# Twenty of the 22 hidden row tiles of a gated feed-forward product computed by Strassen's scheme

## The chip, the cores and the metric

The kernel runs on one core of one Trainium2 chip. The metric is the time of one execution on the device in microseconds (us), as the median of several runs. A difference under about 0.2% (1.6 us) can't be told from no change.

The engines are named as the profile names them: PE is TensorE (matmuls), PEld its weight loads, DVE is VectorE, ACT is ScalarE, POOL is GpSimd, SP is SyncE, whose queue issues most transfers.

## The reference, cut to what matters

One layer of a transformer on 512 tokens of 1024 channels in float32: a mixer of four branches, and then a feed-forward part.

```python
def _swiglu(x, w_in, w_out):
    g, u = jnp.split(x @ w_in, 2, axis=-1)
    return (jax.nn.silu(g) * u) @ w_out

for l in range(DEPTH):
    xn = _rms_norm(h, norm_mix_g[l])
    h = h + _mixer_block(xn, ...)
    h = h + _swiglu(_rms_norm(h, norm_ffn_g[l]), w_ffn_in[l], w_ffn_out[l])
```

`w_ffn_in` is 1024 x 5632 (2816 gate columns, then 2816 up columns), `w_ffn_out` 2816 x 1024. The change touches the feed-forward part alone, and the pools that its tiles lie in.

## The kernel before

Activations stand transposed: 128 channels on the partitions, 512 tokens along. Every float32 operand is kept as two float32r parts, a high one (an ACT copy) and a low one (the source less the high part, on DVE); `split` (lines 119 to 121) makes them. A product of two operands is three matmuls, high by high, high by low, low by high (`mm3`, lines 132 to 134), each of 128 x 128 weights over 512 columns.

All weights of the feed-forward part come as a stream of 128 x 128 units, eight to a chunk of 512 KB, in the order of their use (`unit_stream`, `next_unit`). `load_units` loads a chunk by a transfer on SP's queue (line 146) into one of three `raw` buffers and splits it into `whi` (3 buffers) and `wlo` (2 buffers). Hidden row tile j takes 8 units of the gate columns and 8 of the up columns: 16 units, 48 matmuls.

The mixer ends with `w_out` (line 691); its results are `h1` (tiles `mrg`), and `hg`, which is `h1` times the second norm's gain, in parts (tiles `xg`). The norm itself, `r2`, comes from a sum over channels (`rms`, lines 251 to 261) and is multiplied in only after the products: `gp` by `r2` (line 715), Silu on ACT (716), by `r2` again (717), by `up` (721). So the feed-forward part's matmuls follow those of `w_out` without a wait for `r2`. The 22 row tiles are done in two halves of 11; after each half the eight blocks of `w_ffn_out` take the half's hidden rows (33 matmuls a block) and add to `h1` (731).

The program is written in the order above, and a scheduler then sets the order of each engine's instructions when the program is built. On the chip each engine and each queue takes its instructions in that order. A tile's buffer is taken again when the last reader of the tile before is done; the instruction or transfer that fills it waits for that reader.

Of the kernel before, what the change touches and what calls it, by code (L numbers as in the profile page):

```python
# [29 lines left out]
FH = FK // 2  # L30
# [10 lines left out]
# columns of the packed small parameters  # L41
# [5 lines left out]
# the order of the blocks of forgetting attention's q and k, which VectorE works on for long, and of the convolution  # L47
# [3 lines left out]
def unit_stream():  # L51
    """The 128x128 weight units in the order in which the kernel uses them: (matrix, row tile, column)."""
    s = []

    def block(m, col, ks):
        for k in ks:
            s.append((m, k, col))
# [13 lines left out]
    for half in range(2):  # L71
        ks = range(half * FH, (half + 1) * FH)
        for j in ks:
            block("w_ffn_in", j * P, range(KT))
            block("w_ffn_in", FFN + j * P, range(KT))
        for d in range(KT):
            block("w_ffn_out", d * P, ks)
    return s

# [6 lines left out]
def mixer_kernel(ctx, tc, xT, units, wt1, wt2, wsT, small, out):  # L86
# [5 lines left out]
    slots = ctx.enter_context(tc.tile_pool(name="slots", bufs=1))  # L92
# [3 lines left out]
    BUFS = dict(xg=16, y=18, att=4, aug=6, mrg=8, tmp=6, gt=4)  # L96
# [6 lines left out]
    def slot(tag, dtype=F32):  # L103
        return slots.tile([P, T], dtype, tag=tag, bufs=BUFS[tag], name=nm(tag))
# [62 lines left out]
    # the activation table that Copy and Square are taken from  # L167
# [16 lines left out]
    def x_parts(k):  # L184
        x_k, g = xs[k][:, 0:T], xs[k][:, T:T + 1]
        hi, lo = slot("xg", F32R), slot("xg", F32R)
# [23 lines left out]
    # tri[s, t] = 1 where s <= t  # L210
# [3 lines left out]
    # ntri[s, t] = -1 where s >= t  # L214
# [11 lines left out]
    # mask_sb[k, q] = NEG where k >= q; mask_fx[q, k] = NEG where k > q  # L226
# [10 lines left out]
    # the mean over a head's channels  # L237
# [65 lines left out]
    def token_group(wt, width, nk, banks):  # L303
        """The products of the tokens with a weight of `width` columns; nk row tiles to a chunk."""
        for c in range(KT // nk):
# [3 lines left out]
            lo = wpool.tile([P, nk * width], F32R, tag="wlo", bufs=2, name=nm("wlo"))  # L309
# [9 lines left out]
    def v_parts(banks, first, name):  # L319
        """A head's values in their two parts side by side, so that one product takes both."""  # L320
# [13 lines left out]
    # gmlp's v: gelu, layer norm  # L334
# [22 lines left out]
    # gmlp's causal weights, [s, g, t], kept where s <= t  # L357
# [96 lines left out]
    # log of the forget gate, -softplus(-x), and its sums over the tokens  # L454
# [5 lines left out]
    def values(h, v, wh, wl, w3, dst):  # L460
# [10 lines left out]
        # the lower half has the products of the values' low part  # L471
# [9 lines left out]
    def sb_scores(h):  # L481
# [4 lines left out]
        # both parts of k over the high part of q twice; the high part of k over the low part of q  # L486
# [37 lines left out]
        # in place of row tile 2 its sum with row tile 3, in place of 1 its sum with 2 and 3  # L524
# [7 lines left out]
        # w = exp(z - the sums of softplus over the keys from this one on)  # L532
# [40 lines left out]
    # rows that carry the sums into the products of q and k: 1, 1, F of the query in two parts over  # L573
    # F of the key in two parts, negated, 1, 1
# [19 lines left out]
    def fox_head(h):  # L594
# [4 lines left out]
        # both parts of q over the high part of k twice; the high part of q over the low part of k, and the sums  # L599
# [56 lines left out]
    # sigmoid(x) = (1 + tanh(x / 2)) / 2, of which the last half is taken in at the end  # L656
# [26 lines left out]
    h1, hg = [], []  # L683
    hsum = slot("tmp")
    for d in range(KT):
# [8 lines left out]
        hi, lo = slot("xg", F32R), slot("xg", F32R)  # L694
# [12 lines left out]
    for half in range(2):  # L707
        ks = range(half * FH, (half + 1) * FH)
        a = {}
        for j in ks:  # L710
            gp = bank("g")
            for k in range(KT):
                mm3(gp, next_unit(("w_ffn_in", k, j * P)), hg[k], k == 0, k == KT - 1)
            t = slot("gt")
            V.tensor_tensor(t, gp, r2, op=ALU.mult)  # L715
            S.activation(t, t, AF.Silu)
            V.tensor_tensor(t, t, r2, op=ALU.mult)
            up = bank("g")
            for k in range(KT):
                mm3(up, next_unit(("w_ffn_in", k, FFN + j * P)), hg[k], k == 0, k == KT - 1)  # L720
            V.tensor_tensor(t, up, t, op=ALU.mult)  # L721
            a[j] = tuple(slot("att" if j - ks[0] < 2 else "y", F32R) for _ in range(2))
            split(*a[j], t)
# [13 lines left out]
def pack(inputs):  # L737
    """The inputs in the order in which the program reads them."""
# [50 lines left out]
```

## Time and profile before

| what | value |
|---|---|
| time, median of 3 runs | 824.54 us (823.51 to 824.6) |
| span of the profiled execution, first to last instruction | 821.7 us |
| the rest of the median, before and after the span | 2.8 us |
| PE busy | 816.3 us, 99% of the span |
| DVE, ACT busy | 453.7 us (55%), 322.6 us (39%) |
| POOL busy | 2.4 us |
| bytes moved by transfers | 78.88 MB, mean 96 GB/s |

The profile gives the profiled execution's span; its time as a run isn't listed apart, and the three runs lie 1.8 to 2.9 us above the span. A matmul's shown duration holds its way through the array and overlaps the next one's, so the time that a matmul takes of PE is the distance from its start to the next one's start. DVE's instructions overlap by some 0.08 us in the same way.

### The profile page before, as it was taken

What the parts mean: (1) busy time and instruction counts of PE and PEld (TensorE: products, weight loads), DVE (VectorE), ACT (ScalarE), POOL (GpSimd) and SP (SyncE); (2) the same over time, 40 slices, a digit from 0 to 9 for tenths busy, and PEclk for the clock granted to TensorE, in tenths of its full rate; (3) what the DMA queues carried; (4) which work ended last, traced back from release to release, by engine and by line L of the source; (5) the groups of instructions that cost most, each with busy time, mean ns of one, the idle gap of its engine ahead of it and who ended that gap; (6) DMA issues with size and microseconds to landing.
All of it is one profiled execution on the core that took longest, in us unless ns stands there. A gap on an engine that the chain in (4) does not pass through costs nothing.

```text
span 821.7 us, 9248 instructions
## 1 busy us (share of the span) xinstructions
PE 816.3 (99%) x3653; PEld 658.8 (80%) x3653; DVE 453.7 (55%) x711; ACT 322.6 (39%) x485; POOL 2.4 (0%) x11
## 2 busy tenths in 40 slices
PE   9999999999999999999999999999999999999998
PEld 6888897777788888878888888888888888888886
DVE  8438895776577788756555443444333344344222
ACT  7336337576545455434344432232122233223210
POOL 0000000000000000000000000000000000000000
PEclk9999999999999999999999999999999999999999
DMA  7232321221222222213352223223322222322331
GB/s 286 93 103 91 102 78 58 97 63 66 77 78 80 89 84 69 91 64 103 103 185 85 93 88 102 103 78 102 103 98 83 102 89 92 102 96 84 128 116 39
DMA packets 24091, 78.88 MB, mean 96 GB/s; under 512 B 2672, under 2 KB 2928, under 8 KB 24048
## 3 DMA queue, kind: packets, MB, share of 16 engines
q1 hardware_dynamic: 22608, 75.80, 27.3%
q10 hardware_dynamic: 1440, 2.49, 0.9%
q8 instruction: 29, 0.48, 0.2%
q14 instruction: 14, 0.11, 0.0%
HBM read 76.18 MB, written 2.10 MB: 95 GB/s over the span
## 4 chain that ended last, share of the span: by engine, by line
PE 99%; DVE 0%; DVEq 0%; issue 0%
PE ps L134 30%; PE ps L132 29%; PE ps L133 29%; PE ps L128 1%; PE ps L129 1%; PE ps L130 1%; PE ps L467 1%; PE ps L632 1%; PE ps L502 1%; PE ps L171 0%; PE ps L616 0%; PE ps L469 0%; PE ps L617 0%; PE ps L501 0%; PE ps L537 0%; PE ps L536 0%
## 5 line engine op out<-in xcount | busy, mean ns | idle before, releaser
L132 PE MATMUL ps<-xg,whi 128*128 128x512 f32 x736 | 290.3, 396 | 0.0
L133 PE MATMUL ps<-xg,whi 128*128 128x512 f32 x736 | 289.8, 395 | 0.0
L134 PE MATMUL ps<-xg,wlo 128*128 128x512 f32 x736 | 288.6, 395 | 0.4 <-DVE wlo L121 0.4
L120 ACT ACTIVATE whi<-raw 128x1024 fp32r<-128x1024 f32 (+1 forms) x140 | 144.7, 1034 | 349.5 <-issue 182.2
L121 DVE TENSOR_TENSOR wlo<-raw,whi 128x1024 fp32r<-128x1024 f32 (+1 forms) x140 | 166.4, 1189 | 88.8 <-PE ps L134 68.5
L134 PEld LDWEIGHTS ps<-xg,wlo 128*128 128x128 f32 x736 | 138.3, 188 | 32.6 <-DVE wlo L121 0.8
L132 PEld LDWEIGHTS ps<-xg,whi 128*128 128x128 f32 x736 | 138.5, 188 | 32.1 <-ACT whi L120 0.8
L133 PEld LDWEIGHTS ps<-xg,whi 128*128 128x128 f32 x736 | 138.5, 188 | 31.4 <-issue 0.5
L134 PE MATMUL ps<-y,wlo 128*128 128x512 f32 x256 | 101.1, 396 | 0.0
L132 PE MATMUL ps<-y,whi 128*128 128x512 f32 x256 | 100.8, 394 | 0.3 <-DVE gt L671 0.3
L133 PE MATMUL ps<-y,whi 128*128 128x512 f32 x256 | 101.0, 394 | 0.0
L132 PEld LDWEIGHTS ps<-y,whi 128*128 128x128 f32 x256 | 48.1, 188 | 11.8 <-DVE gt L671 0.8
L134 PEld LDWEIGHTS ps<-y,wlo 128*128 128x128 f32 x256 | 48.1, 188 | 11.2 <-issue 0.3
L133 PEld LDWEIGHTS ps<-y,whi 128*128 128x128 f32 x256 | 48.0, 188 | 11.3 <-issue 0.2
L715 DVE TENSOR_TENSOR gt<-ps,r 128x512 f32<-128x512 f32 x22 | 15.2, 691 | 65.6 <-PE ps L134 63.7
L721 DVE TENSOR_TENSOR gt<-ps,gt 128x512 f32<-128x512 f32 x22 | 15.2, 692 | 65.2 <-PE ps L134 65.2
L662 DVE TENSOR_TENSOR gt<-ps,r 128x512 f32<-128x512 f32 x32 | 22.1, 690 | 25.3 <-PE ps L134 25.3
L663 ACT ACTIVATE gt<-gt 128x512 f32<-128x512 f32 x32 | 20.1, 630 | 37.9 <-DVE gt L662 37.9
L731 DVE TENSOR_TENSOR mrg<-ps,mrg 128x512 f32<-128x512 f32 (+1 forms) x17 | 11.1, 659 | 34.4 <-PE ps L134 34.2
L129 PE MATMUL ps<-whi,xg 128*128 128x512 f32 (+1 forms) x64 | 21.6, 338 | 0.0
L128 PE MATMUL ps<-whi,xg 128*128 128x512 f32 (+1 forms) x64 | 21.5, 338 | 0.0
L130 PE MATMUL ps<-wlo,xg 128*128 128x512 f32 (+1 forms) x64 | 21.3, 337 | 0.0
(229 smaller groups left out, 688.9 us busy)
## 6 DMA issues: line engine op xcount, KB each, us to landing
raw<-units SPq DMA_DIRECT2D x126, 512.0 KB, 3.2
x<-xT SPq DMA_DIRECT2D x8, 256.5 KB, 5.3
raw<-units SPq DMA_DIRECT2D x8, 256.0 KB, 5.3
raw<-wt SPq DMA_DIRECT2D x4, 512.0 KB, 3.2
tmp<-xT ACTq DMA_DIRECT2D x8, 256.0 KB, 4.3
outT<-mrg SPq DMA_DIRECT2D x7, 256.0 KB, 2.0
raw<-wt SPq DMA_DIRECT2D x2, 520.0 KB, 3.2
sml<-small SPq DMA_DIRECT2D x1, 394.0 KB, 5.7
```

Of the source, the lines that this page charges most:

```text
L120: S.activation(dst_hi, src, AF.Copy)
L121: V.tensor_tensor(dst_lo, src, f(dst_hi), op=ALU.subtract)
L128: PE.matmul(out=ps, lhsT=ah, rhs=bh, start=start, stop=False)
L129: PE.matmul(out=ps, lhsT=al, rhs=bh, start=False, stop=False)
L130: PE.matmul(out=ps, lhsT=ah, rhs=bl, start=False, stop=stop)
L132: PE.matmul(out=ps, lhsT=ah, rhs=bh, start=start, stop=False)
L133: PE.matmul(out=ps, lhsT=ah, rhs=bl, start=False, stop=False)
L134: PE.matmul(out=ps, lhsT=al, rhs=bh, start=False, stop=stop)
L662: V.tensor_tensor(t, proj_block(OFF["gate"] + n * D + d * P), r1, op=ALU.mult)
L663: S.activation(t, t, AF.Tanh, scale=0.5)
L715: V.tensor_tensor(t, gp, r2, op=ALU.mult)
L721: V.tensor_tensor(t, up, t, op=ALU.mult)
```

## The change

The gate and up columns of row tiles 2 to 21 are taken two row tiles at a time. For such a pair (a "quad" in the code) the weight is a matrix of 2 x 2 blocks, B11 and B21 the gate columns of the lower and the upper 512 channels, B12 and B22 the up columns. The activations are a 2 x 2 matrix too, by halves of the tokens (256) and halves of the channels. Strassen's scheme in Winograd's form makes the four result blocks from seven block products instead of eight. A block product is 24 matmuls of 256 columns (`product`), so a pair takes 168 matmuls of 256 columns where it took 96 of 512.

The scheme needs sums of blocks. Of the weights, for each pair: t1 = B12 + B11, t2 = t1 + B22, t3 = B12 + B22, t4 = t2 + B21 (the signs of the scheme lie in the activations' sums s1 to s4 and in the subtractions of results). t2 and t4 are made on DVE (`quad_sum`). t1 and t3 are made by two transfers each (`quad_loaded_sum`): SP's queue loads one block into a buffer of the pool `sum`, and when it has landed a transfer from POOL's queue adds the other block to it. All seven operands, summed or not, are then split. Of the activations the sums s1 to s4 and the parts of seven operands (tiles `op`) are made once, ahead of the first pair; they need the normed activations, so `r2` comes in ahead of the products (the tiles A, line 773).

Row tiles 0 and 1 (PLAIN) stay as they were and come first. `w_ffn_out` is now taken in three groups, after 8, 16 and 22 hidden row tiles. `wlo` has 3 buffers instead of 2. The pool `sum` has 6 buffers: the two PLAIN row tiles' hidden parts take two until the first `w_ffn_out` group has read them, and s1 to s4 the other four.

```diff
+PLAIN = 2
+GROUPS = (8, 8, 6)
@@
+def quad_stream():
+    return [(j, half, side) for j in range(PLAIN, FK, 2) for half, side in ((0, 0), (0, 1), (1, 1), (1, 0))]
@@
-                         wpool.tile([P, UNITS * P], F32R, tag="wlo", bufs=2, name=nm("wlo")))
+                         wpool.tile([P, UNITS * P], F32R, tag="wlo", bufs=3, name=nm("wlo")))
@@
+    mix.close()
+    ffn = ctx.enter_context(tc.tile_pool(name="ffn", bufs=1, reuse_waits="tile"))
+    H = T // 2
+    hidden = {}
+    for j in range(PLAIN):
...
+        a = ffn.tile([P, 2, T], F32R, tag="sum", bufs=6, name=nm("plain"))
+        hidden[j] = (a[:, 0], a[:, 1])
+        split(*hidden[j], t)
+    def block4(tag, dtype=F32, bufs=5):
+        return ffn.tile([P, 4, H], dtype, tag=tag, bufs=bufs, name=nm(tag))
+    A = {}
     for half in range(2):
+        A[0, half], A[1, half] = block4("sraw"), block4("sraw")
+        for k in range(4):
+            d = 4 * half + k
+            g = sml[:, C_G2 + d:C_G2 + d + 1]
+            for th in range(2):
+                ts = slice(th * H, (th + 1) * H)
+                V.scalar_tensor_tensor(A[th, half][:, k], h1[d][:, ts], g, r2[:, ts], op0=ALU.mult, op1=ALU.mult)
+    def operand(src):
+        hi, lo = block4("op", F32R, 14), block4("op", F32R, 14)
+        split(hi, lo, src)
+        return hi, lo
+    def combined(a, b, op):
+        t = block4("sum", F32, 6)
+        V.tensor_tensor(t, a, b, op=op)
+        return t
+    o11, o12, o22 = operand(A[0, 0]), operand(A[0, 1]), operand(A[1, 1])
+    s1 = combined(A[1, 0], A[1, 1], ALU.subtract)
+    s2 = combined(s1, A[0, 0], ALU.subtract)
+    s3 = combined(A[0, 0], A[1, 0], ALU.subtract)
+    s4 = combined(A[0, 1], s2, ALU.add)
+    o1, o2, o3, o4 = operand(s1), operand(s2), operand(s3), operand(s4)
+    def quad(c):
+        raw = ffn.tile([P, UNITS * P], F32, tag="sraw", bufs=5, name=nm("sraw"))
+        nc.sync.dma_start(out=raw, in_=quads[c])
+        return raw
+    def quad_sum(a, b):
+        t = ffn.tile([P, UNITS * P], F32, tag="sum", bufs=6, name=nm("sum"))
+        V.tensor_tensor(t, a, b, op=ALU.add)
+        return t
+    def quad_loaded_sum(a, b):
+        t = ffn.tile([P, UNITS * P], F32, tag="sum", bufs=6, name=nm("sum"))
+        nc.sync.dma_start(out=t, in_=quads[a])
+        G.dma_start(out=t, in_=quads[b], accum_op=ALU.add)
+        return t
+    def product(ps, w, x, first=False):
+        (wh, wl), (xh, xl) = w, x
+        for jj in range(2):
+            dst = ps[:, jj * H:(jj + 1) * H]
+            for k in range(4):
+                u = slice((jj * 4 + k) * P, (jj * 4 + k + 1) * P)
+                ends = k == 3 and jj == 1
+                PE.matmul(out=dst, lhsT=wh[:, u], rhs=xh[:, k], start=first and k == 0 and jj == 0, ...)
+                PE.matmul(out=dst, lhsT=wh[:, u], rhs=xl[:, k], ...)
+                PE.matmul(out=dst, lhsT=wl[:, u], rhs=xh[:, k], ...)
+    def quad_rows(j):
+        c = QUADS.index((j, 0, 0))
+        b11, b22, b21 = quad(c), quad(c + 2), quad(c + 3)
+        ra, rc, rb, rd = (bank("a") for _ in range(4))
+        product(ra, quad_parts(b11), o11, True)
+        p1 = slot("tmp")
+        S.activation(p1, ra, AF.Copy)
+        t1 = quad_loaded_sum(c + 1, c)
+        product(rc, quad_parts(t1), o1, True)
+        t2 = quad_sum(t1, b22)
+        product(rb, quad_parts(t2), o2, True)
+        u = slot("tmp")
+        V.tensor_tensor(u, rb, p1, op=ALU.add)
+        product(ra, quad_parts(b21), o12)
...
+        t3 = quad_loaded_sum(c + 1, c + 2)
+        product(rb, quad_parts(t3), o3)
+        v = slot("tmp")
+        V.tensor_tensor(v, rb, p1, op=ALU.add)
...
+        t4 = quad_sum(t2, b21)
+        product(rd, quad_parts(t4), o22, True)
...
+        product(rc, quad_parts(b22), o4)
```

The seven products of a pair are called P1 to P7 below, in this order: B11 by o11, t1 by o1, t2 by o2, B21 by o12, t3 by o3, t4 by o22, B22 by o4. Each pair has further 9 instructions of 512 columns on DVE: u and v, three sums out of PSUM, two products with the gate and two low parts.

The order on three engines, where the first pair begins. On DVE before, behind PLAIN's place, the work of further row tiles follows (`gt` a row tile's gate, `att` and `y` hidden parts):

```order
L715 TENSOR_TENSOR gt_718_3909<-ps_714_3878,r2_3805 128x512
L121 TENSOR_TENSOR wlo_728_3952<-raw_726_3950,whi_727_3951 128x1024
L121 TENSOR_TENSOR att_713_3875<-gt_707_3838,att_712_3874 128x512
L717 TENSOR_TENSOR gt_718_3909<-gt_718_3909,r2_3805 128x512
L721 TENSOR_TENSOR gt_718_3909<-ps_719_3913,gt_718_3909 128x512
L121 TENSOR_TENSOR wlo_733_3987<-raw_731_3985,whi_732_3986 128x1024
```

On DVE now (`sraw_707` to `710` are the four A tiles, `sum_717`, `718`, `719`, `720` are s1 to s4, `op_722` is o1's low part, `sum_739` is the first pair's t1, `sum_742` its t2, `sraw_730` its B22):

```order
L146 TENSOR_TENSOR plain_706_3935<-gt_701_3899,plain_706_3935 128x512
L782 TENSOR_TENSOR sum_718_3972<-sum_717_3970,sraw_707_3938 128x1024
L782 TENSOR_TENSOR sum_719_3974<-sraw_707_3938,sraw_708_3939 128x1024
L146 TENSOR_TENSOR op_722_3979<-sum_717_3970,op_721_3978 128x1024
L782 TENSOR_TENSOR sum_720_3976<-sraw_709_3948,sum_718_3972 128x1024
L146 TENSOR_TENSOR op_724_3983<-sum_718_3972,op_723_3982 128x1024
L146 TENSOR_TENSOR op_726_3987<-sum_719_3974,op_725_3986 128x1024
L146 TENSOR_TENSOR op_728_3991<-sum_720_3976,op_727_3990 128x1024
L801 TENSOR_TENSOR sum_742_4065<-sum_739_4034,sraw_730_3996 128x1024
L146 TENSOR_TENSOR wlo_741_4038<-sum_739_4034,whi_740_4037 128x1024
```

What is new is all of the rows but the first: the activations' sums and splits stand ahead of t2 and of t1's low part. On SP's queue before, each row loads the next chunk when its buffer is free:

```order
L146 DMA raw_715_3879<-units 128x1024 [waits DMAHW2_49,DMAHW6_49,DVE_49,Activation_49]
L146 DMA raw_720_3914<-units 128x1024 [waits DMAHW4_49,DMAHW7_49,DVE_49,Activation_49]
L146 DMA raw_726_3950<-units 128x1024 [waits DMAHW5_49,DVE_49,Activation_49]
L146 DMA raw_731_3985<-units 128x1024 [waits DMAHW1_49,DMAHW6_49,DVE_49,Activation_49]
L146 DMA raw_737_4021<-units 128x1024 [waits DMAHW7_49,DVE_49,Activation_49]
```

On SP's queue now (`sraw_729`, `730`, `731` are B11, B22, B21 of the first pair, `sraw_763`, `764` B11 and B22 of the second, `sum_739` and `sum_750` t1 and t3 of the first, `sum_773` t1 of the second):

```order
L796 DMA sraw_729_3994<-quads 128x1024 [waits PE_49]
L796 DMA sraw_730_3996<-quads 128x1024 [waits DMAHW4_49,DMAHW3_49,DVE_49]
L796 DMA sraw_731_3998<-quads 128x1024 [waits DVE_49,Activation_49]
L796 DMA sraw_763_4233<-quads 128x1024 [waits DVE_49]
L796 DMA sraw_764_4235<-quads 128x1024
L807 DMA sum_739_4034<-quads 128x1024 [waits DMAHW0_49,DVE_49]
L796 DMA sraw_765_4237<-quads 128x1024 [waits DMAHW1_49,DVE_49]
L807 DMA sum_750_4128<-quads 128x1024 [waits DMAHW2_49,DVE_49]
L807 DMA sum_773_4273<-quads 128x1024 [waits DMASW0_49,DVE_49]
```

The load of t1 stands behind the next pair's blocks. `sum_739` lies in the buffer of s1, so its wait for DVE is for the last reader of s1, the row `op_722` above; `sraw_763` waits for s3, the row `sum_719`. `sum_773` lies in the buffer of `sum_739` and waits for the row `wlo_741`. On PE before, plain row tiles follow each other:

```order
L132 MATMUL ps_719_3913<-xg_698_3786,whi_721_3915 128x512
L133 MATMUL ps_719_3913<-xg_699_3787,whi_721_3915 128x512
L134 MATMUL ps_719_3913<-xg_698_3786,wlo_722_3916 128x512
L132 MATMUL ps_725_3949<-xg_642_3500,whi_727_3951 128x512
L133 MATMUL ps_725_3949<-xg_643_3501,whi_727_3951 128x512
```

On PE now, from the end of P1 (`ps_732`) to the begin of P2 (`ps_733`), with two matmuls of P3 (`ps_734`) between:

```order
L825 MATMUL ps_732_4000<-op_711_3958,whi_736_4004 128x256
L826 MATMUL ps_732_4000<-op_712_3959,whi_736_4004 128x256
L827 MATMUL ps_732_4000<-op_711_3958,wlo_737_4005 128x256
L825 MATMUL ps_733_4001<-op_721_3978,whi_740_4037 128x256
L826 MATMUL ps_733_4001<-op_722_3979,whi_740_4037 128x256
L825 MATMUL ps_734_4002<-op_723_3982,whi_743_4067 128x256
L826 MATMUL ps_734_4002<-op_724_3983,whi_743_4067 128x256
L827 MATMUL ps_733_4001<-op_721_3978,wlo_741_4038 128x256
```

Behind P1 nothing stands on PE that doesn't need t1, and 36 matmuls of PLAIN stand between the last matmul of `rms` and P1.

## Rows read from the trace of the kernel before

**Rows 1.** The page, part 1: busy time, share of the span, instructions.

```profile
PE 816.3 (99%) x3653; PEld 658.8 (80%) x3653; DVE 453.7 (55%) x711; ACT 322.6 (39%) x485; POOL 2.4 (0%) x11
```

**Rows 2.** The page, part 4: the chain that ended last, by engine.

```profile
PE 99%; DVE 0%; DVEq 0%; issue 0%
```

**Rows 3.** Busy time by stretch: the feed-forward part, 260-column matmuls, the kernel's start.

```profile
core 0: us, PE busy (x) PEld busy (x) DVE busy (x) ACT busy (x) POOL busy (x), PEclk, DMA share, GB/s
464.00:821.70 357.70, 354.28 (x1532) 287.31 (x1531) 139.81 (x167) 89.64 (x107) 0.00 (x0) 1.00 0.28 94
113.02:122.96 9.94, 9.94 (x85) 9.89 (x84) 9.78 (x12) 2.98 (x6) 0.00 (x0) 1.00 0.32 106
1.20:5.20 4.00, 3.95 (x10) 1.25 (x10) 3.01 (x19) 2.35 (x4) 1.21 (x5) 1.00 0.64 213
```

**Rows 4.** Timeline (start, duration): the norm inside the first row tiles, last matmul.

```profile
463.48 1.06 PE L258 MATMUL ps<-ident,rc 128*128 128x128 f32 x8
464.29 0.48 PE L132 MATMUL ps<-xg,whi 128*128 128x512 f32 x1
...
465.20 0.69 DVE L715 TENSOR_TENSOR gt<-ps,r 128x512 f32<-128x512 f32 x1 [1.93 <-ACT r L261]
...
817.89 0.40 PE L134 MATMUL ps<-y,wlo 128*128 128x512 f32 x1
```

**Rows 5.** Timeline of PE: matmuls of 256 and of 260 columns.

```profile
110.66 0.28 PE L436 MATMUL ps<-big,vg 128*128 128x256 f32 x1
110.77 0.28 PE L437 MATMUL ps<-big,vg 128*128 128x256 f32 x1
110.89 0.28 PE L438 MATMUL ps<-big,vg 128*128 128x256 f32 x1
111.01 0.28 PE L128 MATMUL ps<-whi,xg 128*128 128x260 f32 x1
...
113.02 0.28 PE L129 MATMUL ps<-whi,xg 128*128 128x260 f32 x1
...
122.84 0.28 PE L130 MATMUL ps<-wlo,xg 128*128 128x260 f32 x1
```

**Rows 6.** Groups of weight loads: those of lines 128 to 130, count, mean ns.

```profile
L129 PEld LDWEIGHTS ps<-whi,xg 128*128 128x128 f32 x64 | 12.0, 188 | 1.5
```

**Rows 7.** Timeline of DVE: back-to-back instructions of 256, 512 and 1024 columns.

```profile
71.58 0.87 DVE L353 SCALAR_TENSOR_TENSOR tmp<-tmp,var,sml 128x256 f32<-128x256 f32 x2
72.37 0.75 DVE L354 TENSOR_TENSOR tmp<-tmp,sml 128x256 f32<-128x256 f32 x2
...
74.99 0.68 DVE L401 TENSOR_TENSOR gt<-ps,r 128x512 f32<-128x512 f32 x1
75.59 1.21 DVE L121 TENSOR_TENSOR wlo<-raw,whi 128x1024 fp32r<-128x1024 f32 x1
76.72 0.75 DVE L121 TENSOR_TENSOR vg<-tmp,vg 128x256 fp32r<-128x256 f32 x2
```

**Rows 8.** Groups on ACT: the high part of a chunk.

```profile
L120 ACT ACTIVATE whi<-raw 128x1024 fp32r<-128x1024 f32 x130 | 137.6, 1059 | 342.7 <-issue 182.2 <-PE ps L133 134.4 <-PE ps L129 12.8
```

**Rows 9.** The page, parts 3 and 6: SP's queue; transfers, KB, us to landing.

```profile
q1 hardware_dynamic: 22608, 75.80, 27.3%
...
raw<-units SPq DMA_DIRECT2D x126, 512.0 KB, 3.2
...
sml<-small SPq DMA_DIRECT2D x1, 394.0 KB, 5.7
```

**Rows 10.** Timeline of PE at the kernel's start, after PE stood idle.

```profile
1.25 3.94 PE L171 MATMUL ps<-tmp 128*128 128x512 bf16 x9 [1.25 <-DVE one L166]
```

**Rows 11.** The chain that ended last, its only long pieces not on PE.

```profile
364.92 0.69 DVE gt L671
365.60 1.15 DVE wlo L121
```

More of the change, by code (lines that the diff above doesn't have):

```diff
@@ L70, in unit_stream, with hidden_groups @@
         block("w_out", d * P, range(KT))
[L71 to L75, printed above, removed]
+    for first, n in hidden_groups():
+        if not first:
+            for j in range(PLAIN):
+                block("w_ffn_in", j * P, range(KT))
+                block("w_ffn_in", FFN + j * P, range(KT))
         for d in range(KT):
-            block("w_ffn_out", d * P, ks)
+            block("w_ffn_out", d * P, range(first, first + n))
     return s
+def hidden_groups():
+    first = 0
+    for n in GROUPS:
+        yield first, n
+        first += n
+    assert first == FK
+def quad_stream():
+    return [(j, half, side) for j in range(PLAIN, FK, 2) for half, side in ((0, 0), (0, 1), (1, 1), (1, 0))]
 STREAM = unit_stream()
@@ L103, in slot, with two @@
     def slot(tag, dtype=F32):
-        return slots.tile([P, T], dtype, tag=tag, bufs=BUFS[tag], name=nm(tag))
+        return (keep if tag in KEEP else slots).tile([P, T], dtype, tag=tag, bufs=BUFS[tag], name=nm(tag))
+    def two(dtype=F32R):
+        return keep.tile([P, 2, T], dtype, tag="xg", bufs=8, name=nm("xg"))
     def big(dtype=F32):
@@ L185, in x_parts @@
         x_k, g = xs[k][:, 0:T], xs[k][:, T:T + 1]
-        hi, lo = slot("xg", F32R), slot("xg", F32R)
+        x2 = two()
+        hi, lo = x2[:, 0], x2[:, 1]
         if k:
@@ L704, in mixer_kernel @@
     _, r2 = rms(hsum, "r2")
-    for half in range(2):
[L708 to L723, printed above, removed]
+    mix.close()
@@ new lines, in quad_parts @@
+    def quad_parts(src):
+        hi = wpool.tile([P, UNITS * P], F32R, tag="whi", name=nm("whi"))
+        lo = wpool.tile([P, UNITS * P], F32R, tag="wlo", bufs=3, name=nm("wlo"))
+        split(hi, lo, src)
+        return hi, lo
+    def product(ps, w, x, first=False):
[5 more added lines that the diff above has]
+                ends = k == 3 and jj == 1
+                PE.matmul(out=dst, lhsT=wh[:, u], rhs=xh[:, k], start=first and k == 0 and jj == 0, stop=False, skip_group_check=True)
+                PE.matmul(out=dst, lhsT=wh[:, u], rhs=xl[:, k], start=False, stop=False, skip_group_check=True)
+                PE.matmul(out=dst, lhsT=wl[:, u], rhs=xh[:, k], start=False, stop=ends, skip_group_check=True)
@@ L724, in mixer_kernel @@
+    for first, n in hidden_groups():
+        ks = range(first, first + n)
+        for j in ks[::2]:
+            if j not in hidden:
+                quad_rows(j)
+        last = ks[-1] == FK - 1
         for d in range(KT):
-            ps = bank("a")
+            ps = bank("g")
             for j in ks:
-                mm3(ps, next_unit(("w_ffn_out", j, d * P)), a[j], j == ks[0], j == ks[-1])
-            parts = 2 if half and d == KT - 1 else 1
+                mm3(ps, next_unit(("w_ffn_out", j, d * P)), hidden[j], j == ks[0], j == ks[-1])
+            parts = 2 if last and d == KT - 1 else 1
@@ L731, in mixer_kernel @@
                 V.tensor_tensor(h1[d][:, cs], ps[:, cs], h1[d][:, cs], op=ALU.add)
-                if half:
+                if last:
                     (nc.scalar if i else nc.sync).dma_start(out=out[d * P:(d + 1) * P, cs], in_=h1[d][:, cs])
@@ L748, in pack @@
         units[c, :, j * P:(j + 1) * P] = mats[m][k * P:(k + 1) * P, col:col + P]
+    quads = np.stack([np.concatenate(
+        [w["w_ffn_in"][k * P:(k + 1) * P, side * FFN + jj * P:side * FFN + (jj + 1) * P]
+         for jj in (j, j + 1) for k in range(4 * half, 4 * half + 4)], axis=1) for j, half, side in quad_stream()])
     def cols(*names):
```

46 lines of the change are left out of this document (39 added, 7 removed).

## The prediction

> **What bounds the kernel now.** I read the page's busy line first [rows 1]: PE 99% of 821.7 us, DVE 55%, ACT 39%, POOL nothing. The chain that ended last is PE for 99% [rows 2]; its only long pieces elsewhere are one gate and one split in the mixer, about 1 us of PE's idle time [rows 11]. So the kernel is bound by the number of columns that PE streams, and a change helps as far as it takes columns away without leaving PE to wait. By stretch [rows 3], the feed-forward part is PE without a gap, at a granted clock of 1.00, with DVE busy 139.8 of 357.7 us (39%) and 28% of the transfers' time used. DVE and the queues have room there, but at the part's begin everything that is new hangs on `r2`, which DVE first reads at 465.20 [rows 4].
>
> **Prices.** In the row tiles PE takes a 512-column matmul each (817.89 - 464.29) / 1526 = 0.2317 us [rows 4]. 256-column ones start (111.01 - 110.66) / 3 = 0.117 us apart, 260-column ones (122.84 - 113.02) / 82 = 0.1198 [rows 5]; I take 0.118. DVE from start to start: 0.40 for 256 columns (71.58 to 72.37 for two), 0.60 for 512, 1.13 for 1024 [rows 7]. ACT takes 1.06 for the high part of a chunk [rows 8]. A 512 KB load lands 3.2 us after issue; SP's queue moved 75.80 MB in 27.3% of 821.7 us, 338 GB/s, so 1.55 us of those 3.2 are bytes and 1.65 a fixed part [rows 9].
>
> **Matmuls: -24.2 us.** A pair took 96 x 0.2317 = 22.24 us and takes 168 x 0.118 = 19.82. That is -2.42 a pair, and there are ten pairs. The columns fall by an eighth (96 x 512 to 168 x 256), the time by 10.9%, since a narrow matmul costs a little more than half of a wide one. Everything below is set against this.
>
> **First wait, low part of o11: +3.1.** The PLAIN row tiles cover PE for 36 x 0.2317 = 8.3 us, to 472.6. P1's second matmul reads o11's low part. DVE from 465.2 does one product with `r2` (0.60), 16 products of 256 columns for the tiles A (6.4), two more of 512 (1.20) and two of 1024 (2.26): 475.7. So PE idles 3.1.
>
> **Second wait, t1: +20.0 (15.7 to 25.9).** P1's other 23 matmuls end at 475.7 + 2.7 = 478.4, and by the order on PE nothing else can run that doesn't need t1. The load of t1 takes s1's buffer, whose last reader is `op_722`, in DVE's queue behind the A tiles, 8 rows of 1024 and 8 of 512 in all: 465.2 + 4.8 + 6.4 + 9.0 = 485.4. On SP's queue it stands behind two loads of the next pair, which wait for `sum_719` and go out at 484.3. It lands behind their bytes at 484.3 + 1.65 + 3 x 1.55 = 490.6, or at 488.6 if it doesn't share with them. Then POOL's transfer adds the other block. No row shows such a transfer. From below it is bounded by a plain load, 3.2; from above by twice the 5.7 us of the slowest landing of such a size [rows 9], 11.4. I take 5.5: the fixed part and the bytes twice, since it must read what it adds to, is 1.65 + 2 x 1.55 = 4.75, and other loads run beside it. A plain load is the nearest row, so I stay nearer to it. t1 stands at 496.1; t2 on DVE and t1's low part take 1.13 each, to 498.4. From 478.4 that is 20.0 us of idle PE. With 3.2 and 488.6 it is 15.7, with 11.4 it is 25.9.
>
> The Trainium skill, "DMA: Bandwidth & Descriptors", section "Anatomy of one DMA", fits a transfer issued from GpSimd with 2.0 us and the bytes at 436 GB/s; an estimate from it is 3.2 us for 512 KB, by which this wait would be 17.7 and the whole kernel about 824. The same page's "Rules for kernel authors" says that an accumulating transfer reads its destination and writes it later, which speaks against taking it for a plain one. No row here shows either.
>
> **Third wait, the second pair's t1: +2.3 (0.1 to 8.2).** That load takes the first t1's buffer when its low part is made, 498.4; load and adding are 3.2 + 5.5, to 507.1. On DVE the second pair's t2 (1.13) stands ahead of u (0.60), which frees the PSUM bank that the first pair's t3 product takes; that is 508.8. PE has P2 to P4 (72 x 0.118 = 8.5 us, a few of them done ahead of t1's low part) until 506.5. PE is slower for a while after an idle stretch: nine matmuls at the kernel's start took 3.94 us, 0.438 each instead of 0.2317 [rows 10], so a few us of cold matmuls lie inside this wait and are no term of their own.
>
> **Fourth wait, behind the first `w_ffn_out` group: +3.6 (1.1 to 9.5).** The load of the t1 after next wants a buffer that a PLAIN row tile's hidden part holds until that group's last matmul. From there 0.2 + 3.2 + 5.5 = 8.9, and three rows of DVE (3.4) ahead of what PE needs: 12.3. PE has P1 to P3 and a little, 8.7. The third group needs no such buffer.
>
> **In the steady pairs: 0, but narrowly.** A pair's t1 load, its adding transfer and the six 1024-column and six 512-column rows of DVE that stand in that ring make 8.9 + 6.8 + 3.6 = 19.3 us, against 19.82 of PE. Above an adding transfer of about 6.0 every us costs one per pair, for nine pairs. DVE has 9 x 1.13 + 9 x 0.60 = 15.6 us per pair, 79%; ACT seven splits (7.4) and about five narrower ones, under 13 us; transfers seven of 512 KB, five plain (7.75 us) and two adding. None of them is the bound by itself.
>
> **Costed at nothing.** The third `w_ffn_out` group's eight extra sums (0.60 each on DVE) lie under blocks of 24 x 0.2317 = 5.56 us. Behind the last pair's P7 the program has 32 matmuls of earlier hidden row tiles (7.4 us), under which its last hidden parts are made (one row of 1024 at most and four of 512 on DVE, about 3.5 us; that is what they would cost uncovered). `wlo`'s third buffer and the pools by tiles touch the mixer only at its 1 us of waits [rows 11]: 0, within 1 either way.
>
> **The sum.** -24.2 + 3.1 + 20.0 + 2.3 + 3.6 = +4.8 against the span of 821.7: 826.5. The median of before lies 2.8 above its span, so 829.3.
>
> **Rivals.**
> *The adding transfer costs no more than a plain one, and the kernel is faster.* Then the third wait is gone but for the cold matmuls, which it no longer covers, 9 x (0.438 - 0.2317) = 1.9, and the waits are 3.1 + 15.7 + 1.9 + 1.1 = 21.8. The sum is -2.4: 822.1. From an adding transfer of about 3.5 us down, with t1's load not held by its neighbours, the sign turns. For it: bytes are idle 72% of the time [rows 3]. Against: what it has to read twice.
> *The ring binds.* At 8 us the waits are 3.1 + 22.5 + 4.8 + 6.1 = 36.5 and the ring adds 2.0 x 9 = 18: +30.3, 854.8. For it: the margin is only half a us a pair. Against: most of the 3.2 us of a landing is fixed part, which needn't double. At 11.4 it would be 5.9 x 3 of waits and 5.4 x 9 of ring above my forecast, about 895.
> *PE doesn't go faster with narrow matmuls, since a weight load takes longer than one.* A weight load is shown as 0.188 us [rows 6]; a matmul of 256 columns that waits for its load would take 0.225 us, 0.118 plus the 0.107 that 128 columns take by the same pitch, and 1680 of them 180 us more: about 1010. Against it: in the stretch of 260 columns 84 loads of 0.188 us (15.8 us) lie within 9.94 us, and the matmuls start 0.1198 apart [rows 3, 5, 6], so loads overlap both matmuls and each other.
>
> The Trainium skill, "TensorE: Matmul & The Clock Gate", Part 3, "The mechanism", holds that a weight load runs beside matmuls in flight only where it takes another row group of the array; all of this kernel's take the whole array, so by it the last rival would come true. The trace disagrees: 0.1198 us apart with a load for every matmul.
>
> **How the numbers follow.** The forecast (adding transfer 4 to 6.5 us) has 0.5, the plain price 0.27, the binding ring 0.16, the weight loads 0.01, anything else 0.06. A measurement of this kernel can tell about 0.2%, 1.6 us, from no change: faster is below 822.9, slower above 826.2. At an adding transfer of 4 the waits are 3.1 + 18.5 + 1.9 + 2.1 = 25.6, 825.9 in all; at 6.5 there are 3 more of waits and 4.5 of ring, 836.8. So 0.44 of the forecast's 0.5 is slower and 0.06 the same. Of the plain price 0.21 is faster and 0.06 the same (with t1's load behind its neighbours it is about 824). Of the rest 0.04 is faster, by waits shorter than I summed them, 0.01 the same, and 0.18 slower with the ring and the weight loads. Faster 0.25, the same 0.13, slower 0.62. The range reaches down to the plain price with 6 us less of waits, a third of the second one (816), and up to an adding transfer of 7.5: 829.3 + 3 x 2.0 + 9 x 1.5 = 848.8, so 850.
>
> **What would show it.** Right: matmuls of 256 columns 0.117 to 0.120 us apart in the pairs; one gap of PE of about 20 us behind P1 near 478, ended by the split of t1, with lower granted clock behind it; gaps of 2 to 4 us at the first pair's t3 product and in the pair behind the first `w_ffn_out` group; the adding transfer landing some 5.5 us after issue; DVE about 79% busy in the pairs, PE without gaps from the third pair on. Wrong: a spacing of 0.13 or more (0.01 us is 17 us in all); gaps in every pair, ended by the adding transfer (the ring); no long gap behind P1; waits in the mixer other than those of before.

## The result

| what | before | after |
|---|---|---|
| time, median of 4 runs | 824.02 us (823.49 to 824.6) | 850.33 us (847.83 to 855.28) |
| span of the profiled execution | 821.7 us | 846.1 us |
| PE, DVE, ACT, POOL busy | 816.3, 453.7, 322.6, 2.4 us | 802.1, 542.2, 366.9, 19.8 us |

The ratio is 1.0329, with a 95% interval from 1.0303 to 1.0355: slower by 3.3%. The forecast was 829.3 us. Its sign was right, its size was not: 5 us of loss were forecast, 26 came, and the time lies at the end of the range (850) and just outside it.

The page of the changed kernel, its parts 1 (busy), 4 (the chain that ended last) and 6 (transfers, with the median us from issue to landing), against [rows 1, 2, 9]:

```profile
PE 802.1 (95%) x4373; PEld 683.1 (81%) x4373; DVE 542.2 (64%) x806; ACT 366.9 (43%) x532; POOL 19.8 (2%) x31
...
PE 27%; DMA 4%; DVE 2%; issue 1%; DVEq 0%; POOLq 0%
...
raw<-units SPq DMA_DIRECT2D x86, 512.0 KB, 3.4
sraw<-quads SPq DMA_DIRECT2D x30, 512.0 KB, 4.3
sum<-quads SPq DMA_DIRECT2D x20, 512.0 KB, 3.7
sum<-quads POOLq DMA_DIRECT2D x20, 512.0 KB, 5.6
```

PE was 99% busy and is 95% busy. Its busy time fell by 14 us, and its idle time rose by 39. The chain as shown covers only 34% of the span. Adding transfers and the DVE rows behind them now stand in the chain, and the adding transfer's median is 5.6 us, where the sum had taken 5.5.

Where PE waits is read from the starts of its matmuls. Timeline of PE in the changed kernel, the rows around its longest gaps (start, duration, then what ended the idle time):

```profile
473.99 0.28 PE L825 MATMUL ps<-op,whi 128*128 128x256 f32 x1
477.03 0.38 PE L826 MATMUL ps<-op,whi 128*128 128x256 f32 x1 [2.76 <-DVE op L146]
...
479.76 0.28 PE L827 MATMUL ps<-op,wlo 128*128 128x256 f32 x1
499.97 0.58 PE L825 MATMUL ps<-op,whi 128*128 128x256 f32 x1 [19.93 <-ACT whi L145]
...
511.88 0.28 PE L826 MATMUL ps<-op,whi 128*128 128x256 f32 x1
514.78 0.38 PE L825 MATMUL ps<-op,whi 128*128 128x256 f32 x1 [2.61 <-DVE tmp L841]
...
556.60 0.28 PE L827 MATMUL ps<-op,wlo 128*128 128x256 f32 x1
561.81 0.55 PE L825 MATMUL ps<-op,whi 128*128 128x256 f32 x1 [4.92 <-DVE tmp L841]
...
640.36 0.28 PE L826 MATMUL ps<-op,whi 128*128 128x256 f32 x1
641.87 0.39 PE L827 MATMUL ps<-op,wlo 128*128 128x256 f32 x1 [1.23 <-DVE wlo L146]
```

There are smaller ones of the last kind at 661.87 and 682.90 (1.0 each), one at 535.92 (0.8), and one of 3.4 at 705.42, where an output group's weight split stands on DVE behind the last t2. The account, each gap less the pitch of one matmul:

| item | forecast | measured |
|---|---|---|
| matmuls, ten pairs | -24.2 | -23.7 (mean pitch 0.1183 us) |
| `r2` first read (466.49, was 465.20) | 0 | +1.3 |
| first wait, o11's low part | +3.1 | +2.9 |
| second wait, t1 | +20.0 | +20.1 |
| from there to the first pair's u (behind the second's t2) | +2.3 | +6.1 (3.3 slow or halting matmuls, 2.8 idle) |
| slow matmuls behind that | 0 | +1.6 |
| u of the second and of the third pair (535.92, 556.60) | 0 | +0.7, +5.1, and 2.6 of slow matmuls |
| fourth wait, behind the first output group | +3.6 | 0 |
| second group's pairs | 0 | +3.2, and 3.1 at 705.42 |
| sum | +4.8 | +23.0 |

Of the 18.2 us between the two sums, 14.7 lie in the pairs, which were costed at nothing, and 3.8 behind P2's begin; the fourth wait's 3.6 go the other way. The span rose by 24.4; 1.4 us are not assigned. The rest of the 26 is that the profiled execution was the fastest of the four: its run took 847.83 us.

### The profile page after: what moved, and what is told of

It is laid out like the page before. It is cut to its first block, busy times and chain, and to the rows that moved or that the text cites. A ratio compares the mean times of both kernels' runs of the same rounds, so it can differ in the third digit from the quotient of the medians.

```text
span 846.1 us, 10945 instructions
## 1 busy us (share of the span) xinstructions
PE 802.1 (95%) x4373; PEld 683.1 (81%) x4373; DVE 542.2 (64%) x806; ACT 366.9 (43%) x532; POOL 19.8 (2%) x31
## 5 line engine op out<-in xcount | busy, mean ns | idle before, releaser
L159 PE MATMUL ps<-xg,wlo 128*128 128x512 f32 x576 | 226.0, 397 | 3.0 <-DVE wlo L146 3.0
L158 PE MATMUL ps<-xg,whi 128*128 128x512 f32 x576 | 227.0, 396 | 0.0
L157 PE MATMUL ps<-xg,whi 128*128 128x512 f32 x576 | 226.2, 395 | 0.5 <-ACT whi L145 0.5
L825 PE MATMUL ps<-op,whi 128*128 128x256 f32 x560 | 160.3, 287 | 28.5 <-ACT whi L145 20.5
L145 ACT ACTIVATE whi<-raw 128x1024 fp32r<-128x1024 f32 (+2 forms) x100 | 102.1, 1023 | 167.7 <-PE ps L158 120.2
L826 PE MATMUL ps<-op,whi 128*128 128x256 f32 x560 | 160.1, 286 | 2.8 <-DVE op L146 2.8
L827 PE MATMUL ps<-op,wlo 128*128 128x256 f32 x560 | 159.2, 287 | 2.7 <-DVE wlo L146 2.7
L146 DVE TENSOR_TENSOR wlo<-raw,whi 128x1024 fp32r<-128x1024 f32 (+2 forms) x100 | 117.8, 1179 | 56.7 <-ACT whi L145 56.1
L825 PEld LDWEIGHTS ps<-op,whi 128*128 128x128 f32 x560 | 109.0, 195 | 29.9 <-ACT whi L145 21.0
L159 PEld LDWEIGHTS ps<-xg,wlo 128*128 128x128 f32 x576 | 108.2, 188 | 28.4 <-DVE wlo L146 3.7
L157 PEld LDWEIGHTS ps<-xg,whi 128*128 128x128 f32 x576 | 108.3, 188 | 24.9 <-ACT whi L145 1.0
L158 PEld LDWEIGHTS ps<-xg,whi 128*128 128x128 f32 x576 | 108.2, 188 | 25.0 <-issue 1.0
L826 PEld LDWEIGHTS ps<-op,whi 128*128 128x128 f32 x560 | 108.4, 194 | 3.3 <-DVE op L146 3.1
L827 PEld LDWEIGHTS ps<-op,wlo 128*128 128x128 f32 x560 | 107.8, 194 | 3.5 <-DVE wlo L146 3.3
L157 PE MATMUL ps<-y,whi 128*128 128x512 f32 x112 | 44.0, 397 | 0.8 <-DVE gt L688 0.8
L158 PE MATMUL ps<-y,whi 128*128 128x512 f32 x112 | 44.4, 396 | 0.0
```

The source lines that it names most:

```text
L145: S.activation(dst_hi, src, AF.Copy)
L146: V.tensor_tensor(dst_lo, src, f(dst_hi), op=ALU.subtract)
L157: PE.matmul(out=ps, lhsT=ah, rhs=bh, start=start, stop=False)
L158: PE.matmul(out=ps, lhsT=ah, rhs=bl, start=False, stop=False)
L159: PE.matmul(out=ps, lhsT=al, rhs=bh, start=False, stop=stop)
L825: PE.matmul(out=dst, lhsT=wh[:, u], rhs=xh[:, k], start=first and k == 0 and jj == 0, stop=False, skip_group_check=True)
```

## The experiments

The question was which of the waits hang on the adding transfer, which on the buffer that t1 takes, and which on DVE. Times below are spans of profiled executions, beside medians where several runs were made.

**The first pair's t1 in another buffer.**

```diff
-    def quad_loaded_sum(a, b):
+    def quad_loaded_sum(a, b, early=False):
...
-        t = ffn.tile([P, UNITS * P], F32, tag="sum", bufs=6, ...)
+        t = (wpool.tile([P, UNITS * P], F32, tag="raw", bufs=3, ...) if early else
+             ffn.tile([P, UNITS * P], F32, tag="sum", bufs=6, ...))
...
-        t1 = quad_loaded_sum(c + 1, c)
+        t1 = quad_loaded_sum(c + 1, c, j == PLAIN)
```

> Only the first pair's t1 is loaded and added in a `raw` buffer, which is free before `r2`, in place of s1's buffer. Theory (the wait behind P1 is set by when t1's buffer comes free, not by the adding transfer alone): the gap of 20.2 us behind P1 falls to about 12.5, what DVE's queue still needs ahead of t1's low part; the second pair's t1 starts earlier too, so the gap of 2.9 near 512 us and 1.6 us of slow matmuls behind it go; span 846.1 - 12 = 834. The gaps behind the first output group (5.2) and near 640 to 705 stay. Rival (DVE's queue sets the entry anyway, t1's transfers are hidden): gap still 18 to 20 us, span 844 to 846.

Span 834.1, the fastest of the four; median 840.06, ratio 1.0177 (1.0141 to 1.0213). The one gap of 20 us became several short ones, of 2.0, 2.9 and three of 0.7 to 1.1 us, and the longer of them end by rows of DVE and ACT for the activations' operands. The first wait grew from 3.0 to 4.2, and some 45 matmuls around them were 0.213 us apart. So the buffer of s1 held t1 back, as in the prediction's second wait. The gaps of 2.6 near 501 and 4.0 near 547 stayed, against the theory's hope for the first of them, and those of the second group too. These runs spread from 835.78 to 849.14.

**Every pair's t1 there.** The same edit, with `True` for `j == PLAIN`.

> t1 of every pair is loaded and added in a `raw` buffer; t3 stays in the pool `sum`. Theory (in the steady pairs the ring t1's load, adding transfer, t2, last read of the buffer takes 21.0 us against 19.9 of PE; cut it and no wait is left): gaps near 640, 662, 683 and 705 (6.9 in all) and the 5.2 behind the first output group gone, with the 2.6 us of slow matmuls behind that; with the first pair's as in the run before, span about 819. Rival (what fills the ring is the transfers' contention for the engines of the queues, busy 86% there, so they only wait elsewhere): gaps of about 1 us a pair stay, span 827 or more.

Span 825.6, median 822.93, ratio 0.999 (0.998 to 0.9999). From 520 us on no gap is left but one of 2.3 at an output group, so the ring was real and hung on t1's buffer. The profiled execution was the slowest of the ten (827.35); its span is 6.6 us above the 819 expected, the median some 2. The excess lies at the entry: t3's adding transfer met other loads there. That transfer, and what the transfers' engines did from 500 to 506 us (the columns are as in [rows 3]):

```profile
sum<-quads POOLq DMA_DIRECT2D x1, 512.0 KB, 9.0
```

```profile
500.00:506.00 6.00, 1.72 (x15) 1.51 (x13) 0.02 (x1) 1.11 (x2) 0.86 (x1) 0.89 1.05 249
```

The transfers' engines were busy the whole time (1.05) while PE waited 5.5 us. The rival's contention is there too, then, but PE waits for it at the entry, not in the ring.

**No adding.** `G.dma_start(out=t, in_=quads[b], accum_op=ALU.add)` left out, so t1 and t3 are B12 alone.

> The adding transfers are left out, t1 and t3 are plain loads of B12 (so the sums are not made). Theory (the adding transfer's 5.5 us lie on the path at the entry, behind the first group and in the ring): gap behind P1 20.2 - 5.6 = 14.6, the gaps near 512, 557 and 640 to 705 gone and the slow matmuls behind the first two with them; span 846 - 25 = 821. Rival (the ring is bound by its order on DVE and PE, not by the transfer): only 5.6 us at the entry go, span 838 to 840. Also, if the adding transfers make the spread of the times (847.8 to 855.3), it falls to about 1 us.

Span 819.4, median 821.59, ratio 0.9969 (0.9956 to 0.9982). The gap behind P1 is 13.2 and no later one is over 1 us. The runs lie within 0.8 us.

**The sums on DVE.**

```diff
-        t1 = quad_loaded_sum(c + 1, c)
+        b12 = quad(c + 1)
+        t1 = quad_sum(b12, b11)
...
-        t3 = quad_loaded_sum(c + 1, c + 2)
+        t3 = quad_sum(b12, b22)
```

> t1 and t3 are made on DVE from B12 loaded once per pair into an `sraw` buffer; no adding transfer, four loads a pair in place of five and two adding ones. DVE has 11 x 1.14 + 9 x 0.60 = 17.9 us a pair against 19.9 of PE. Theory (transfers, not DVE, are what PE waits for): gap behind P1 about 13 us, no other gap, span about 820. Rival (DVE is the next bound: 90% busy in a fixed order): gaps of 1 to 2 us in each pair, span 830 to 840.

Span 829.1, median 830.86, within 1.7 us. The gap behind P1 is 12.4, and nearly each pair has a gap of about 1 us. They are not DVE's: the row of ACT that ends the one near 640.1 is a weight block's high part, which begins when PE has left the buffer it goes to, and PE goes on when it is done (pieces of the chain: start, duration, what):

```profile
640.06 1.07 ACT whi L145
641.17 0.39 PE ps L825
```

So theory and rival were both partly wrong: the pairs have gaps, and by this chain they come from the three `whi` buffers. No run with a fourth one tested that. Ten of them make 9 us; with the entry they outweigh the gain.

**Matmuls that nothing reads, in the second wait.**

```diff
+FILL = 84
...
+        if j == PLAIN:
+            for _ in range(FILL):
+                PE.matmul(out=rd, lhsT=o11[0][:, 0, 0:P], rhs=o11[1][:, 0:2]..., start=True, stop=True)
         t1 = quad_loaded_sum(c + 1, c)
```

> As the changed kernel, with 84 matmuls of 512 columns that nothing reads put on PE between P1 and P2 of the first pair (84 x 0.232 = 19.5 us, as long as the wait). Theory (PE is slow behind the wait because it stood idle): P2 begins at the same time, and the 25 matmuls 0.213 us apart behind it are 0.118 apart, so 3.0 us go; the slow ones behind the waits at 512 and 557 us stay; span about 843. Rival (they are slow by their weights or by the transfers that run then): still 0.213 apart, span 846.

Timeline of PE, where P2 begins and where it waits next:

```profile
501.68 0.39 PE L826 MATMUL ps<-op,whi 128*128 128x256 f32 x1 [0.42 <-ACT whi L146]
501.90 0.28 PE L827 MATMUL ps<-op,whi 128*128 128x256 f32 x1
502.02 0.28 PE L828 MATMUL ps<-op,wlo 128*128 128x256 f32 x1
502.14 0.28 PE L826 MATMUL ps<-op,whi 128*128 128x256 f32 x1
...
510.19 0.28 PE L827 MATMUL ps<-op,whi 128*128 128x256 f32 x1
516.47 0.58 PE L826 MATMUL ps<-op,whi 128*128 128x256 f32 x1 [6.00 <-DVE tmp L845]
```

P2's matmuls are 0.118 apart at once, so those at 0.213 come from the idle time. But P2 began 1.7 us later than in the changed kernel, and the span, of a single run, is 846.7: PE only came earlier to the next wait, now 6.3 us long. Slow matmuls ahead of a wait that ends by transfers cost nothing, as the prediction had it for this place. Those behind 514.78 and 561.81 stand ahead of no such cover.

**POOL's transfers without adding**: the same transfers, with `accum_op` left off, so that they write over.

> As the changed kernel, but POOL's transfers write B11 and B22 over instead of adding them (t1 and t3 are not sums). Theory (adding costs because the bytes count twice): they land 3.2 to 3.7 us after issue instead of 5.6, the gap behind P1 falls by 2, the ring to about 19 us, so no gaps at 640 to 705; span about 832. Rival (a transfer from POOL's queue costs so much whether it adds or not): 5.6 us to landing, span 846.

The page's row of transfers, against the 5.6 above:

```profile
sum<-quads POOLq DMA_DIRECT2D x20, 512.0 KB, 3.9
```

The gap behind P1 fell to 17.7, and no gap of 1 us is left behind it. The span (a single run) is 824.7, 7 us better than expected, since the wait near 557 and the slow matmuls behind it went as well. So POOL's queue alone does not take the ring over PE's time: without the 1.7 us that adding costs, the ring fits.

**t3 without adding.** Only t3's adding transfer left out.

> As the changed kernel, but t3 is a plain load of B12 (its adding transfer is left out); t1's load and adding transfer stay as they are, in their buffers. In the ring of the steady pairs t1's load takes about 5.05 us from issue to the begin of the adding, where a load by itself takes 3.2. Theory (t3's adding transfer, which runs at the same time, slows it): the load falls to 3.2 to 3.7, the ring to 10.5 + 3.5 + 5.4 = 19.4 us, below PE's 19.9, so no gaps of 1.0 us at 640, 662 and 683; the gap of 20.2 behind P1 and the one of about 5 behind the first group stay; span about 836. Rival (the `sraw` load issued 1.7 us ahead of it on the same queue slows it): load still about 5, ring 20.9, gaps stay, span 845.

The span, 836.0 in a single run, is what the theory gave, but the theory is wrong: the ring's gaps of 1.2 at 654 and 675 stayed, t1's load took 4.5 us from issue to the adding one's, and that one 6.1. Most of the gain is the gap near 557 (0.7 instead of 5.2) with its slow matmuls. What slows t1's load is on SP's queue beside it, as the rival says of the ring, though not of the span. How much of the gain is the edit's stays open: an execution of the changed kernel itself came to a span of 840.1 (below).

**B22 and B21 loaded once for all pairs**, so that t1's load and adding transfer have few neighbours.

```diff
-        b11, b22, b21 = quad(c), quad(c + 2), quad(c + 3)
+        b11 = quad(c)
+        if not kept:
+            kept.extend((quad(c + 2), quad(c + 3)))
+        b22, b21 = kept
```

> As the changed kernel with both adding transfers, but B22 and B21 are loaded for the first pair alone and used for all pairs (the weights of the others are so not the reference's): three loads a pair and two adding transfers in place of five and two; DVE, ACT and PE do what they did. Theory (plain loads that run at the same time stretch the ring's load from 3.2 to 5 to 7 us and its adding transfer from about 5 to 5.3 to 7.7): load 3.2 to 3.7, adding 4.8 to 5.4, ring 18.5 to 19.6 us, below PE's 19.9, no gaps from 530 us on; the entry's 20 us stay; span 829 to 832, and the runs lie within 3 us. Rival (the adding transfers and t1's and t3's loads hinder each other): the gaps of 5 near 557 and 1.0 to 3.4 at 640 to 705 stay, span 842 or more, spread as before.

Pieces of its chain in the second group (start, duration, what):

```profile
638.95 3.25 DMA sum<-quads
642.27 0.49 issue
642.76 5.22 DMA sum<-quads
...
662.32 3.35 DMA sum<-quads
665.74 0.49 issue
666.23 5.09 DMA sum<-quads
```

The prices are the theory's: 3.3 and 5.2 us without neighbours. The time is not: span 841.1, median 843.99, with gaps of 2 to 3 us. The scheduler set the rows in another order here: DVE's row that frees t1's buffer begins 13.0 us behind t2's sum instead of 9.3, which is more than the transfers lost. The run shows what neighbours do to the transfers; what the ring would take with them gone and its order kept stays worked out, not shown.

**Four plain row tiles.** `PLAIN = 4`, nine pairs, and the third and fourth tile's hidden parts in `two()` instead of the pool `sum`. Once with t1 in `sum`, as in the changed kernel:

> Four plain row tiles and nine pairs, but t1 in the pool `sum` as in the changed kernel. Theory (entry and ring are two separate losses): the entry's 29 us of waits and slow matmuls fall by about 20, the waits behind the first group and in the ring stay (5 to 8 and about 1 a pair and 3 before an output group); span 824 to 828, as long as before. Rival (with the entry covered the ring has slack from then on): no waits in the pairs, span 806.

Span 819.3, median 821.92, ratio 0.9988 (0.9963 to 1.0012): no different from before. The gap behind P1 is 6.8, and those of the ring stay (0.8 to 2.1). And once with t1 in `raw`:

> t1 in `raw` buffers as in e2_t1_raw, and four plain row tiles instead of two (the hidden parts of the third and fourth in `xg` buffers), nine pairs instead of ten. PE has 22.3 us more of plain matmuls behind `r2`, while DVE makes the activations' sums. Theory (the entry's waits, 18 us, and 5.7 us of slow matmuls of e2_t1_raw are the time from `r2` to the sums and to t3): they fall below 3 us in all, nine pairs bring 9 x 2.4 = 21.8, span about 803, ratio to before 0.978. Rival (each further pair's t3 keeps PE waiting under contention): 5 to 8 us of waits stay, span 808 to 812.

Its page, part 1, and the feed-forward part by stretch (columns as in [rows 3]):

```profile
PE 796.7 (99%) x4301; PEld 674.9 (84%) x4301; DVE 536.2 (67%) x800; ACT 363.3 (45%) x528; POOL 18.1 (2%) x29
```

```profile
464.00:803.00 339.00, 334.98 (x2186) 304.54 (x2184) 222.41 (x256) 130.58 (x150) 15.76 (x18) 1.00 0.48 140
```

Span 803.0, median 805.27, ratio 0.9788 (0.9773 to 0.9804). PE is 99% busy again, at a granted clock of 1.00 throughout, and its longest gap in this part is 0.7. This version beats both kernels. Entry and ring were two losses: with the entry covered by plain work alone, the ring's gaps stayed. Either edit alone brings the kernel back to the time of before, both bring it 18.6 us below. Their gains of 27.4 and 28.4 us do not add up to the 45.1 of both, since t1's buffer shortens the entry too.

**The changed kernel twice more**, for the spread of its times.

> The changed kernel once more, unaltered, for a second profile: its runs spread from 847.8 to 855.3 us. Theory (the spread comes from how t1's load and adding transfer meet other loads, which shifts from run to run): the gaps of the first profile at 474 (3.0) and 480 (20.2) within 0.3 us, those of the later pairs (2.9, 0.8, 5.2, 1.5, 1.0, 1.0, 3.4) redistributed, their sum 12 to 20 us; adding transfers either 5.3 to 5.7 us or 7 to 8. Rival (the entry, or PE's clock, makes the spread): the entry's gap differs by over 1 us and the later ones don't.

> As e12_again, a third profile of the changed kernel: if the spread lies in the transfers of the later pairs, the gaps at 474 and 480 are again 3.0 and 20.2 within 0.3 us and the later ones sum to 12 to 20 us in another distribution.

Spans 846.4 and 840.1. P2 began at 500.13 and 499.98 us (499.97 in the first profile), so the entry is the same to 0.2 us. The gaps of the later pairs summed to 15.3 and 12.1 (15.9 before), in other sizes and partly in other places. So the spread lies in the ring and in the matmuls behind its gaps: from P2's begin on, the three profiles last 346.2, 346.3 and 340.1 us, and of the 6 us between them some 3 to 4 are gaps and most of the rest matmuls at the lower granted clock. The times were 848.13 and 841.82; all six executions of this kernel reach from 841.8 to 855.3, with a median of 848.3, so a difference of a few us between single runs tells nothing, and those above are read by their gaps. In one of the two the gap behind P1 was shown as 18.3 instead of 20.2, with slow matmuls ahead of it and the same end.

## Why the prediction came out as it did

**What held.** The pitch of narrow matmuls (0.118 taken, 0.1183 measured), the first wait (3.1, 2.9) and the second (20.0, 20.1) came out as summed from [rows 4, 7, 9] and the order, in spite of the adding transfer, which no row of before had. Taking it at the fixed part and twice the bytes, rounded up to 5.5, was about right for one that runs by itself (5.3 for the last pair's, with no load beside it).

The second wait's 20.1 is in part luck. Pieces at its end:

```profile
493.23 1.01 POOL L808 DMA_DIRECT2D sum<-quads  x1 [421.55 <-DMA sum<-quads]
...
498.86 1.06 ACT L145 ACTIVATE whi<-sum 128x1024 fp32r<-128x1024 f32 x1 [9.84 <-DMA sum<-quads]
```

Reckoned from `r2`, t1 stood 1.4 us later than forecast, since its load took 5.8 beside the next pair's loads and 0.6 passed to POOL's issue. Against that, PE went on when ACT had made t1's high part, 1.2 us behind t1, and not after two rows of DVE (2.26). Two matmuls later it stood idle again, for 0.5 us, which the table counts in the next wait.

By the Trainium skill, "DMA: Bandwidth & Descriptors", section "Anatomy of one DMA", an estimate for these 512 KB is 3.2 us. The runs show 5.3 for a lone one with adding and 3.4 for a lone one without.

The rival of the weight loads fell: 1680 loads of 0.19 us lie under matmuls 0.118 apart. Its price was also summed wrongly: by the pitch it names, 128 columns take 0.059 us and not 0.107, which makes 99 us more and not 180; at a chance of 0.01 that moved nothing. The rule of the Trainium skill named there ("TensorE: Matmul & The Clock Gate", Part 3, "The mechanism") disagrees with this trace as with that of before.

**The step that failed** is "In the steady pairs: 0, but narrowly". The ring was found, and its 10.4 us of DVE rows were right. Its transfers were mis-sized: they were priced as if alone, 3.2 + 0.2 + 5.5 = 8.9, and took 10.5 in a steady turn, 13.7 and 14.3 in the two worst. One turn of the ring as measured, from SP's, POOL's and DVE's timelines: t1's load goes out, the adding transfer goes out, t2's sum begins, the next t1's load goes out:

```profile
670.42 0.33 SPq L807 DMA_DIRECT2D sum<-quads  x1
...
675.47 0.86 POOL L808 DMA_DIRECT2D sum<-quads  x1 [8.06 <-DVE tmp L848]
...
680.92 1.23 DVE L801 TENSOR_TENSOR sum<-sum,sraw 128x1024 f32<-128x1024 f32 x1 [3.92 <-DMA sum<-quads]
...
691.45 0.33 SPq L807 DMA_DIRECT2D sum<-quads  x1
```

That is 5.05 + 5.45 + 10.53 = 21.03 us, against 168 x 0.1183 = 19.9 of PE, and so the gaps of 1.0 us a pair. (The row of POOL names DVE's L848 because that ended last before it; in the program the adding transfer waits for its load.) Of the 5.05, the load, priced at 3.2, is 4.5:

```profile
sum<-quads SPq DMA_DIRECT2D x1, 512.0 KB, 4.5
```

Some 0.55 is the way from its landing to POOL's issue, priced at 0.2. The adding transfer's 5.45 is what was forecast. Against the forecast, then, these turns ran over by the load beside other loads and by the way to POOL. Twice it was worse. The answers for single transfers of the changed kernel: an adding one that goes out at 675.47, the one of the fourth pair's t1 at 551.05 with the load that went out beside it, and the load of that t1 from 544.95:

```profile
sum<-quads POOLq DMA_DIRECT2D x1, 512.0 KB, 5.4
```

```profile
sraw<-quads SPq DMA_DIRECT2D x1, 512.0 KB, 3.9
sum<-quads POOLq DMA_DIRECT2D x1, 512.0 KB, 7.6
```

```profile
sum<-quads SPq DMA_DIRECT2D x1, 512.0 KB, 5.5
```

Of the 20 adding transfers 12 took 5.3 to 5.7 us, one 6.4, and seven 7.0 to 7.9. Here 5.5 + 0.6 + 7.6 = 13.7 took the place of 8.9, which makes 4.8 of the gap of 5.2 at 556.60. The prediction had allowed for neighbours at the entry ("behind their bytes") and not in the ring, although it had counted seven transfers a pair.

**The third wait** failed by the same term: the second pair's adding transfer, at 504.94, took 7.9 instead of 5.5, beside a load that went out 0.3 us ahead of it. **The slow matmuls** were rightly no term behind the second wait, since the third covers them, but there were two more places, 4.2 us in all.

**The fourth wait** did not come. The prediction let the load go out at the output group's last matmul. The plain tiles' parts are read for the last time some 4.4 us ahead of the group's end, since matmuls of other hidden row tiles stand behind them: the load went out at 612.84, the group's last matmul at 617.27, t2's sum began at 621.88, and PE had no gap from 610 to 640. Those 4.4 us are more than the 3.6 forecast.

**The rivals.** The nearest to what came is the binding ring, put at 854.8 with a chance of 0.16: right in its place and in its total, wrong in its reason, since an adding transfer by itself is not 8 us. The plain price is what POOL's transfers without adding show: 826.5 in one run, where the rival gave 822.1; they took 3.9 and not 3.2.

## What to carry to other kernels

A ring of transfer, transfer and vector work that just fits into the time of the engine it feeds may well not fit (here 19.3 of 19.8 us as forecast, 21.0 of 19.9 as measured): price each of its transfers as it runs among the other loads of the same stretch, and forecast from that, not from the median of lone ones. Look which tile's last reader frees the buffer of the first load in such a ring; moving that one load to another pool was worth 27 us at the entry and in the ring together (850.33 to 822.93). And where a stage needs operands that come late, plain work ahead of it pays more than one more unit of the cheaper work: two plain row tiles in place of one pair cost 2.4 us of matmuls and brought 17.7 net (822.93 to 805.27).

## What the runs showed of the hardware that was not expected

- An adding transfer of 512 KB from POOL's queue took 5.3 us with no load beside it, where the last one without adding took 3.4. The longer times go with a plain load that goes out at nearly the same time: in the three profiles of the changed kernel the 17 with one within 0.6 us of their issue took 6.4 to 8.2 us. Of the other 43, 37 took 5.0 to 5.8, though loads that went out 0.7 us or more apart ran beside most of them. Four of the last six (6.4 to 7.2) went out 2.1 to 2.7 us from the other adding transfer. No run changed the moment of issue alone, so that it is the cause is not shown.
- From the landing of a load on SP's queue to the issue of POOL's transfer that waits for it go 0.53 to 0.71 us, mostly 0.56.
- Behind 20.1 us of idle time PE's granted clock was 0.50, that is 1.2 GHz, until 505.95, with matmuls of 256 columns 0.213 us apart; behind 5.1 us of it, at 561.81, until 567.39. Behind the 2.9 us near 512 it was 0.50 too, from 516.19 to 519.60. Behind the 3.0 us at 474 it stayed at 1.00 in the first profile and fell to 0.50 in several later profiles with the same gap, one of them of the same kernel. The idle time alone does not settle it, and what does stays open.
